# New issue-order tables for all five queues of a hybrid decoder step on one core

## The chip, the core and the metric

The kernel runs on one NeuronCore of one Trainium2 chip. The metric is device time in microseconds of one execution; a version is given by the median of its runs. Five engines with queues of their own work side by side: TensorE (PE in the profile), VectorE (DVE), ScalarE (ACT), GpSimd (POOL) and SyncE (SP), which here issues nearly all DMAs. Each works through its queue strictly in order: an instruction that waits for its input holds up everything behind it on that engine.

## The reference, cut to what matters

One layer of a decoder, in float32: 2048 prompt tokens and 8 single decode tokens, model width 1024.

```python
z = einsum(rmsnorm(x, norm1_g), w_in)            # 1024 -> 1792
xr, gr, q, k, v = split(z)
xc = causal_conv(xr)                             # width 4
hs = rglru(xc)                                   # gated linear recurrence, a scan over tokens
rec = hs * gelu(gr)
att = sliding_window_attention(q, k, v, sinks)   # window 128, 8 heads, 2 KV heads
mix = concat(rmsnorm(rec, rec_norm_g), rmsnorm(att, attn_norm_g))
h = x + einsum(mix, w_out)
hn = rmsnorm(h, norm2_g)
y = h + einsum(silu(einsum(hn, w_gate)) * einsum(hn, w_up), w_down)   # 1024 -> 2816 -> 1024
out = rmsnorm(y, final_norm_g)
```

Outputs are the normalized tokens, the last keys and values, and the states of convolution and recurrence.

## The kernel before

**Numbers.** Every product is made three times at TensorE's reduced-precision float32: high part by high part, high by low and low by high. So each operand exists as hi and lo: ACT casts the high part (for weights L1044, L1904, L1973), and POOL or DVE subtracts it from the original to get the low part (L1045, L1905, L1974). Activations get theirs the same way.

**Stage 1** (to about 650 us) takes the prompt in four sub-blocks of 520 and three times 512 tokens. For each: the norm (`xn`, L1106 and L1107), the input projection in 14 units of 128 columns (`ip`), the convolution (L1458), the recurrence with tanh gates (`g` on PE, `ra` and `ia` L1479 on ACT, then L1489 to L1501), the gelu gate (`gt`, L1518 to L1521), and attention: scores `s`, softmax (L1640 to L1651), transpositions of the probabilities `pt`, their hi and lo parts `pth` (ACT L1661) and `ptl` (DVE L1662), and the product `o`. The two group norms spread their factors over the partitions with small matmuls `bc_at` and `bc_rc`, whose result ACT copies out (`rb_at`, L1141); such a matmul needs the one PSUM bank for small things. The output projection `op` and the sums into the residual (`xres`, L1763) follow. ACT's square root and its exponential family live in different function tables, so a `ACT_TABLE_LOAD` stands between them.

**Stage 2** (from about 650 us) is the feed-forward part in three groups of tokens (2 × 344, 2 × 342, 2 × 342), each in 11 steps over slices of the hidden width. A step multiplies 2 × 2 blocks with seven products in place of eight, gate (`ps_g`), up (`ps_u`) and down (`pw`). Several products share a PSUM bank: before the next product may add to it, ACT (copies `c_u`, L2111, L2116, L2118) or DVE (`c_u`, L2090) must have read what is there. The sums into y are DVE's L2176. At a group's end comes the final norm: the row of factors is transposed on PE (`tr_f`), copied by ACT (L1150), written to HBM (`rows_f`, L1151) and read back spread over all partitions (`rb_f`, L1157); DVE multiplies y by it (L2196, 16 steps for a group), SP writes the result (`out_yT`, L2197), and the next group's y is loaded into the space that comes free (L1900). All of this runs while the next group's first products are on PE.

**The order.** The program is written as chains of steps, and each instruction is recorded under a key (the engine and the chain for DVE, ACT, POOL and SP, the PSUM tile for PE). A table of strings, `ORDER`, one string for each engine, then lists these keys in the order in which the engine shall issue them: `u2_1_5:12` is the next twelve matmuls of product 5 of the up part, group 2, step 1, and `pu1.1+1` is the second one still left of its chain. `order_engines()` reads the tables and ties each instruction to the one ahead of it, with no semaphore: only the order in the queue is bound.

```python
def order(runs, todo):
    last = None
    for run in runs.split():
        key, _, at = run.partition("+")
        key, _, n = key.partition(":")
        for _ in range(int(n or 1)):
            r = todo[key].pop(int(at or 0))
            if last is not None:
                tc.add_manual_dep(r, last.name, no_sync, reason="issue order")
            last = r
```

The data dependences, and the semaphores that come of them, are the same for every order. The tables also say how many warm-up matmuls stand in front (`w_st_x0:17`).

## Time and profile before

| | us |
|---|---|
| three runs | 2012.89, 2016.06, 2016.81 (median 2016.06) |
| the profiled execution | 2014.07 |
| its span, first to last instruction | 2012.3 |
| TensorE busy in it | 1981.0 (98%) |
| VectorE / ScalarE / GpSimd busy | 1562.8 / 979.2 / 960.3 |
| mean granted TensorE clock | 0.992 |

The profiled execution is one more than the three runs; it lies 1.99 us below their median. The page gives busy times, and names for each idle stretch of an engine what ended it ("<-DVE y L2176": a sum of VectorE at line 2176). Names there are those of the program without buffer numbers. The granted clock is that of TensorE; 1.00 is full speed. "PEld" is TensorE's loading of weights, which overlaps its products.

### The profile page before, as it was taken

What the parts mean: (1) busy time and instruction counts of PE and PEld (TensorE: products, weight loads), DVE (VectorE), ACT (ScalarE), POOL (GpSimd) and SP (SyncE); (2) the same over time, 40 slices, a digit from 0 to 9 for tenths busy, and PEclk for the clock granted to TensorE, in tenths of its full rate; (3) what the DMA queues carried; (4) which work ended last, traced back from release to release, by engine and by line L of the source; (5) the groups of instructions that cost most, each with busy time, mean ns of one, the idle gap of its engine ahead of it and who ended that gap; (6) DMA issues with size and microseconds to landing.
All of it is one profiled execution on the core that took longest, in us unless ns stands there. A gap on an engine that the chain in (4) does not pass through costs nothing.

```text
span 2012.3 us, 34843 instructions
## 1 busy us (share of the span) xinstructions
PE 1981.0 (98%) x12106; PEld 1882.1 (94%) x12106; DVE 1562.8 (78%) x2894; ACT 979.2 (49%) x2029; POOL 960.3 (48%) x822
## 2 busy tenths in 40 slices
PE   9999999999999999999999999999999999999997
PEld 9988888888877999999999999999999999999997
DVE  7877986777896889889888786886568586766775
ACT  6775674564663544444446433433345333433433
POOL 5512452130232886788889754544456423322323
PEclk9999999999999999999999999999999999999998
DMA  9864675586688978566668786776557775565552
GB/s 319 301 231 132 208 273 197 173 265 209 214 293 276 334 254 272 210 217 223 237 234 285 252 295 226 242 235 205 191 191 268 225 254 199 178 212 192 184 182 93
DMA packets 218471, 461.93 MB, mean 230 GB/s; under 512 B 26231, under 2 KB 90407, under 8 KB 218279
## 3 DMA queue, kind: packets, MB, share of 16 engines
q1 hardware_dynamic: 214662, 456.69, 67.8%
q10 hardware_dynamic: 3632, 3.02, 0.5%
q8 instruction: 95, 1.56, 0.3%
q14 instruction: 82, 0.66, 0.1%
HBM read 345.51 MB, written 115.17 MB: 229 GB/s over the span
## 4 chain that ended last, share of the span: by engine, by line
PE 91%; DVE 5%; DMA 2%; ACT 1%; issue 1%; POOL 0%; SPq 0%; DVEq 0%; ACTq 0%; POOLq 0%
PE ps_u L1071 21%; PE ps_g L1071 21%; PE pw L1071 18%; PE ip L1071 13%; PE op L1071 8%; PE pd L1071 4%; PE o L1071 1%; PE s L1071 1%; PE pt L1076 1%; PE g L1071 1%; DMA rb_f<-rows_f 0%; DVE y L2196 0%; DMA rb_x<-rows_x 0%; DVE xn L1107 0%; DVE y L2245 0%
## 5 line engine op out<-in xcount | busy, mean ns | idle before, releaser
L1071 PE MATMUL ps_g<-hn,w_g 128*128 128x342 f32 (+1 forms) x2772 | 570.2, 320 | 0.2 <-DVE c_u L2090 0.2
L1071 PE MATMUL ps_u<-hn,w_u 128*128 128x342 f32 (+1 forms) x2772 | 563.1, 321 | 3.3 <-ACT c_u L2111 3.2
L1071 PEld LDWEIGHTS ps_u<-hn,w_u 128*128 128x128 f32 x2772 | 462.6, 190 | 4.4 <-ACT c_u L2111 3.5
L1071 PEld LDWEIGHTS ps_g<-hn,w_g 128*128 128x128 f32 x2772 | 461.2, 188 | 1.6 <-issue 0.4
L2176 DVE TENSOR_TENSOR y<-y,pw 128x342 f32<-128x342 f32 (+1 forms) x756 | 358.5, 505 | 115.4 <-PE pw L1071 109.3
L1071 PE MATMUL ip<-xn,w_in 128*128 128x512 f32 (+1 forms) x1680 | 366.0, 358 | 2.5 <-ACT xn L1106 1.4
L1071 PEld LDWEIGHTS ip<-xn,w_in 128*128 128x128 f32 x1680 | 271.0, 190 | 43.3 <-ACT xn L1106 1.6
L1071 PE MATMUL pw<-fh,wd 128*128 128x342 f32 (+1 forms) x864 | 253.9, 320 | 0.1
L1071 PE MATMUL pw<-t,wd 128*128 128x342 f32 (+1 forms) x972 | 243.3, 320 | 4.6 <-DVE y L2176 3.9
L1071 PE MATMUL op<-mix,w_out 128*128 128x512 f32 (+1 forms) x960 | 208.4, 358 | 0.0
L1071 PEld LDWEIGHTS op<-mix,w_out 128*128 128x128 f32 x960 | 159.5, 191 | 24.7
L1071 PEld LDWEIGHTS pw<-t,wd 128*128 128x128 f32 x972 | 169.8, 188 | 6.1 <-DVE y L2176 5.1
L1974 POOL TENSOR_TENSOR wd<-rd,wd 128x512 fp32r<-128x512 f32 x85 | 121.0, 1423 | 101.9 <-ACT wd L1973 100.8
L1071 PEld LDWEIGHTS pw<-fh,wd 128*128 128x128 f32 x864 | 158.8, 189 | 0.9 <-DVE y L2176 0.3
L1973 ACT CAST wd<-rd 128x512 fp32r<-128x512 f32 x159 | 98.4, 620 | 120.4 <-PE ps_u L1071 44.2
L1905 POOL TENSOR_TENSOR w_u<-ru,w_u 128x512 fp32r<-128x512 f32 x44 | 60.5, 1375 | 172.1 <-ACT w_u L1904 156.9
L1071 PE MATMUL pw<-fl,wd 128*128 128x342 f32 (+1 forms) x432 | 132.7, 320 | 0.0
L2072 POOL TENSOR_TENSOR c_u<-c_u,c_g 128x342 f32<-128x342 f32 (+1 forms) x60 | 65.2, 1088 | 133.1 <-DVE c_u L2090 120.4
L2090 DVE TENSOR_TENSOR c_u<-c_u,ps_u 128x342 f32<-128x342 f32 (+1 forms) x99 | 50.3, 508 | 98.0 <-PE ps_u L1071 97.5
L2061 DVE TENSOR_TENSOR fl<-c_u,fh 128x342 fp32r<-128x342 f32 (+1 forms) x132 | 102.5, 781 | 17.4 <-ACT fh L2060 16.7
L2060 ACT CAST fh<-c_u 128x342 fp32r<-128x342 f32 (+1 forms) x132 | 63.1, 480 | 107.5 <-POOL c_u L2072 43.3
L1904 ACT CAST w_g<-rg 128x512 fp32r<-128x512 f32 x99 | 60.9, 621 | 70.9 <-issue 26.0
(319 smaller groups left out, 3528.2 us busy)
## 6 DMA issues: line engine op xcount, KB each, us to landing
w_g<-split_g SPq DMA_DIRECT2D x88, 512.0 KB, 4.3
w_u<-split_u SPq DMA_DIRECT2D x88, 512.0 KB, 4.6
w_in<-split_w SPq DMA_DIRECT2D x84, 512.0 KB, 3.7
rg<-in_wgate SPq DMA_DIRECT2D x110, 256.0 KB, 3.0
ru<-in_wup SPq DMA_DIRECT2D x110, 256.0 KB, 3.1
w_out<-split_w SPq DMA_DIRECT2D x48, 512.0 KB, 4.4
split_g<-w_g SPq DMA_DIRECT2D x44, 512.0 KB, 3.5
split_u<-w_u SPq DMA_DIRECT2D x44, 512.0 KB, 3.3
```

The source lines that it names most:

```text
L1071: r = nc.tensor.matmul(*args, **kw)
L1076: r = nc.tensor.transpose(*args)
L1904: nc.scalar.copy(w[:, 0, :], src)
L1905: lo_eng.tensor_tensor(w[:, 1, :], src, w[:, 0, :].bitcast(F32), op=ALU.subtract)
L1973: nc.scalar.copy(w[:, :, 0], v)
L1974: eng((E_DLO0, E_DLO1, E_DLO2)[gi][j]).tensor_tensor(w[:, :, 1], v, w[:, :, 0].bitcast(F32), op=ALU.subtract)
L2060: nc.scalar.copy(hi, v)
L2061: nc.vector.tensor_tensor(lo, v, hi.bitcast(F32), ALU.subtract)
L2072: (nc.vector if p == NPAIR - 1 or src is not v else eng(E_MUL[2 * h + n])).tensor_tensor(v, src, g, op=ALU.mult)
L2090: nc.vector.tensor_tensor(o, a, b, op)
L2176: nc.vector.tensor_tensor(v, v, ps, ALU.add)
```

## The change

Only the strings of `ORDER` are replaced, all five of them. The words that come with the change say that they were made with lengths out of four traces, with the table loads of ScalarE and the landings of factor rows (`rb_f` and the like) taken into account. Every instruction of before is there again; the new file is three lines shorter, so its line numbers are lower by three (L2108 is L2111 of before). Long stretches are in the same order as before, among them 150 to 200, 1000 to 1050 and 1200 to 1550 us on PE, and nearly all of the end. What moves lies in 0 to 100, 200 to 260, 550 to 700, 800 to 1000, 1090 to 1170 and about 1600 us.

Two lines of PE's string at about 1600 us, out of 166,000 characters of difference:

```diff
-g2_1_4:9 u2_1_2:11 tr_f1_0 u2_1_2 u2_1_6:12 w2_0_2_0:3 u2_1_7:11 u2_1_5:12 u2_1_7 w2_0_6_0:3 u2_1_4:12 u2_1_3:12
...
+g2_1_4:3 u2_1_1:11 g2_1_4:9 u2_1_2:11 tr_f1_0 u2_1_2 u2_1_6:12 w2_0_2_0:3 u2_1_7:11 u2_1_5:12 u2_1_7 u2_1_3:12
+u2_1_4:7 g2_2_1 u2_1_4 g2_2_1 u2_1_4:4 w2_0_6_1:3 w2_0_6_0:3 g2_2_1:7 w2_0_1_3:2 g2_2_2 w2_0_1_3 g2_2_1:2 g2_2_2
```

The strings themselves tell little; the rows below tell what stands in the queues.

**The border of the first and second group, about 1150 us.** ScalarE before; c_g and c_u are blocks of the gate and up part, ps_u1_1_1 is the bank that the up part's first product fills, wd and w_u are high parts of weights, t1 is a high part for the down product:

```order
L2069 ACTIVATE c_g1_1_10_7476<-ps_g1_1_1_13521 128x342
L2060 CAST t1_0_7472<-c_u1_0_11_7471 128x342
L2060 CAST t1_1_7473<-c_u1_0_10_7470 128x342
L1973 CAST wd1_0_4_13813<-sd0_4_13793 128x2x256
L1973 CAST wd1_0_3_13766<-rd1_0_3_13727 128x2x256
L2111 COPY c_u1_1_10_7488<-ps_u1_1_1_13752 128x342
L1973 CAST wd1_0_6_13902<-rd1_0_6_13772 128x2x256
L2116 COPY c_u1_1_01_7487<-ps_u1_1_1_13752 128x342
```

And after:

```order
L2066 ACTIVATE c_g1_1_10_7476<-ps_g1_1_1_13521 128x342
L2108 COPY c_u1_1_10_7488<-ps_u1_1_1_13752 128x342
L1970 CAST wd1_0_4_13813<-sd0_4_13793 128x2x256
L1970 CAST wd1_0_3_13766<-rd1_0_3_13727 128x2x256
L2057 CAST t1_1_7473<-c_u1_0_10_7470 128x342
L1970 CAST wd1_0_6_13902<-rd1_0_6_13772 128x2x256
L2113 COPY c_u1_1_01_7487<-ps_u1_1_1_13752 128x342
```

The copy of the first up product (c_u1_1_10, L2111, now L2108) moved from behind the casts of wd1_0_4 and wd1_0_3 to ahead of them, right behind the step that reads the gate's bank; the cast of t1_1 moved behind them.

VectorE at the same border before; y0_4 and so on are the first group's results, rb_f0_1 the row of factors of its second half:

```order
L2090 TENSOR_TENSOR c_g1_1_11_7477<-c_g1_1_11_7477,ps_g1_1_1_13521 128x342
L2196 SCALAR_TENSOR_TENSOR y0_4_8343<-y0_4_8343,vec_102,rb_f0_1_13615 128x344
L2196 SCALAR_TENSOR_TENSOR y0_1_8276<-y0_1_8276,vec_102,rb_f0_1_13615 128x344
L2196 SCALAR_TENSOR_TENSOR y0_3_8312<-y0_3_8312,vec_102,rb_f0_1_13615 128x344
L2196 SCALAR_TENSOR_TENSOR y0_5_8360<-y0_5_8360,vec_102,rb_f0_1_13615 128x344
L2196 SCALAR_TENSOR_TENSOR y0_1_8276<-y0_1_8276,vec_102,rb_f0_1_13615 128x344
L2196 SCALAR_TENSOR_TENSOR y0_1_8276<-y0_1_8276,vec_102,rb_f0_0_13645 128x344
L2090 TENSOR_TENSOR c_g1_1_01_7475<-c_g1_1_01_7475,ps_g1_1_5_13593 128x342
L2196 SCALAR_TENSOR_TENSOR y0_3_8312<-y0_3_8312,vec_102,rb_f0_0_13645 128x344
L2196 SCALAR_TENSOR_TENSOR y0_4_8343<-y0_4_8343,vec_102,rb_f0_0_13645 128x344 x2
L2196 SCALAR_TENSOR_TENSOR y0_3_8312<-y0_3_8312,vec_102,rb_f0_1_13615 128x344
```

And after:

```order
L2087 TENSOR_TENSOR c_g1_1_11_7477<-c_g1_1_11_7477,ps_g1_1_1_13521 128x342
L2058 TENSOR_TENSOR t1_0_7472<-c_u1_0_11_7471,t1_0_7472 128x342
L2058 TENSOR_TENSOR t1_1_7473<-c_u1_0_01_7469,t1_0_7472 128x342
L1902 TENSOR_TENSOR w_u1_1_2_13684<-ru1_1_01_13588,w_u1_1_2_13684 128x512
L2193 SCALAR_TENSOR_TENSOR y0_5_8360<-y0_5_8360,vec_102,rb_f0_1_13615 128x344
L2193 SCALAR_TENSOR_TENSOR y0_3_8312<-y0_3_8312,vec_102,rb_f0_1_13615 128x344
L2193 SCALAR_TENSOR_TENSOR y0_4_8343<-y0_4_8343,vec_102,rb_f0_1_13615 128x344
L2193 SCALAR_TENSOR_TENSOR y0_1_8276<-y0_1_8276,vec_102,rb_f0_1_13615 128x344
L2193 SCALAR_TENSOR_TENSOR y0_3_8312<-y0_3_8312,vec_102,rb_f0_1_13615 128x344
L2087 TENSOR_TENSOR c_g1_1_01_7475<-c_g1_1_01_7475,ps_g1_1_5_13593 128x342
L2193 SCALAR_TENSOR_TENSOR y0_1_8276<-y0_1_8276,vec_102,rb_f0_1_13615 128x344
L2193 SCALAR_TENSOR_TENSOR y0_1_8276<-y0_1_8276,vec_102,rb_f0_0_13645 128x344
```

Three steps (the low parts t1_0, t1_1 and w_u1_1_2) now stand ahead of the first multiplication by rb_f0_1; before, they stood behind 11 (t1_1), 12 (w_u1_1_2) and 14 (t1_0) of these multiplications, below the piece shown. The sum c_g1_1_01 comes after five of the multiplications instead of six.

**The recurrence of the second sub-block, about 250 us.** ScalarE before; the two table loads are those for the square root (L1496) and back to tanh and exponentials (L1479), ra1_2 is the tanh gate that frees the bank of g1_2:

```order
L1470 CAST xch1_2_3046<-xc1_2_2940 128x512
L1044 CAST w_out0_4_1_3372<-raw_out0_4_1_3370 128x512
L1117 ACTIVATE sq_h0_2_3431<-xres0_2_3234 128x520
L1044 CAST w_out0_5_0_3436<-raw_out0_5_0_3434 128x512
L1673 COPY ratt_150<-o5_0_2964 64x4x128
L1661 CAST pth5_1_0_2500<-pt5_1_0_2495 128x512
L1044 CAST w_out0_5_1_3442<-raw_out0_5_1_3440 128x512
L1620 CAST qst7_1_2607<-qraw_148 64x512
L1479 ACT_TABLE_LOAD
L1479 ACTIVATE ra1_2_3044<-g1_2_0_0_3050,hab_154 128x512
```

And after:

```order
L1467 CAST xch1_2_3046<-xc1_2_2940 128x512
L1670 COPY ratt_150<-o5_0_2964 64x4x128
L1658 CAST pth5_1_0_2500<-pt5_1_0_2495 128x512
L1103 ACTIVATE xn2_5_3680<-xs2_5_3678,vec_102 128x512
L1114 ACTIVATE sq_h0_2_3431<-xres0_2_3234 128x520
L1041 CAST w_out0_5_0_3436<-raw_out0_5_0_3434 128x512
L1476 ACT_TABLE_LOAD
L1476 ACTIVATE ra1_2_3044<-g1_2_0_0_3050,hab_154 128x512
L1103 ACTIVATE xn2_6_3685<-xs2_6_3683,vec_102 128x512
L1041 CAST w_out0_5_1_3442<-raw_out0_5_1_3440 128x512
L1617 CAST qst7_1_2607<-qraw_148 64x512
```

The casts of w_out0_5_1 and qst7_1 moved from ahead of the second table load to behind the tanh; the square sq_h0_2 and the cast of w_out0_5_0 moved behind the copies of the attention unit (L1673 and L1661, now L1670 and L1658).

**The border of the second and third group, about 1605 us.** TensorE before; pw2_0_1_0 is a bank of the down product, w_u2_1_3 and w_u2_1_4 are weights of the third and fourth product of the up part:

```order
L1071 MATMUL ps_u2_1_5_18816<-hn2_1_2_17945,w_u2_1_5_18714 128x342 x3
L1071 MATMUL ps_u2_1_1_18695<-hn2_1_4_17961,w_u2_1_7_18754 128x342
L1071 MATMUL pw2_0_1_0_18675<-t2_0_7652,wd2_0_1_18624 128x342 x3
L1071 MATMUL ps_u2_1_1_18695<-hn2_1_8_18012,w_u2_1_4_18833 128x342 x4
L1071 MATMUL ps_u2_1_1_18695<-hn2_1_9_18021,w_u2_1_4_18833 128x342
L1071 MATMUL ps_u2_1_1_18695<-hn2_1_8_18012,w_u2_1_4_18833 128x342
L1071 MATMUL ps_u2_1_1_18695<-hn2_1_9_18021,w_u2_1_4_18833 128x342 x3
L1071 MATMUL ps_u2_1_1_18695<-hn2_1_10_18043,w_u2_1_4_18833 128x342 x3
L1071 MATMUL ps_u2_1_5_18816<-hn2_1_5_17980,w_u2_1_3_18794 128x342 x3
```

And after:

```order
L1068 MATMUL ps_u2_1_5_18816<-hn2_1_2_17945,w_u2_1_5_18714 128x342 x3
L1068 MATMUL ps_u2_1_1_18695<-hn2_1_4_17961,w_u2_1_7_18754 128x342
L1068 MATMUL ps_u2_1_5_18816<-hn2_1_5_17980,w_u2_1_3_18794 128x342 x3
L1068 MATMUL ps_u2_1_5_18816<-hn2_1_6_17987,w_u2_1_3_18794 128x342 x4
L1068 MATMUL ps_u2_1_5_18816<-hn2_1_7_17991,w_u2_1_3_18794 128x342
L1068 MATMUL ps_u2_1_5_18816<-hn2_1_6_17987,w_u2_1_3_18794 128x342
L1068 MATMUL ps_u2_1_5_18816<-hn2_1_7_17991,w_u2_1_3_18794 128x342 x3
L1068 MATMUL ps_u2_1_1_18695<-hn2_1_8_18012,w_u2_1_4_18833 128x342 x4
L1068 MATMUL ps_u2_1_1_18695<-hn2_1_9_18021,w_u2_1_4_18833 128x342
L1068 MATMUL ps_u2_1_1_18695<-hn2_1_8_18012,w_u2_1_4_18833 128x342
L1068 MATMUL ps_u2_1_1_18695<-hn2_1_9_18021,w_u2_1_4_18833 128x342
```

The twelve matmuls with w_u2_1_3 and the twelve with w_u2_1_4 now stand ahead of the three of pw2_0_1_0, which follow seven rows below the piece shown.

## The prediction

> **What bounds the kernel now.** I read the page's head first, then what TensorE (PE) waited for, then fifty-microsecond windows, and last the timeline around each wait.

> ```profile
> span 2012.3 us, 34843 instructions
> PE 1981.0 (98%) x12106; PEld 1882.1 (94%) x12106; DVE 1562.8 (78%) x2894; ACT 979.2 (49%) x2029; POOL 960.3 (48%) x822
> ```

> TensorE is busy for 1981.0 of 2012.3 us. The change keeps all instructions, so it can only win from the 31.3 us in which PE has nothing to do, and from time at a lowered clock. PE's waits, with total, number and longest:

> ```profile
> PE pw L1071 <- DVE y L2176: 3.9, 2, 3.2
> PE ps_u L1071 <- ACT c_u L2111: 3.2, 1, 3.2
> PE g L1071 <- ACT ra L1479: 2.7, 1, 2.7
> ...
> PE pt L1076 <- DVE ptl L1662: 1.8, 2, 1.6
> PE bc_at L1071 <- ACT rb_at L1141: 1.8, 1, 1.8
> PE ip L1071 <- ACT xn L1106: 1.4, 1, 1.4
> ```

> Five of these lie in the middle of the run, each at one place with at most a small second one; the last is the start. The windows show the place and the clock (columns: window, length, busy time of PE, PEld, DVE, ACT, POOL with counts, granted PE clock, DMA share, GB/s):

> ```profile
> 200.00:250.00 50.00, 48.25 (x313) 43.56 (x311) 46.45 (x73) 35.88 (x68) 20.14 (x18) 0.97 0.61 206
> 250.00:300.00 50.00, 47.06 (x320) 43.16 (x319) 41.80 (x81) 37.42 (x76) 25.40 (x25) 0.97 0.79 271
> 600.00:650.00 50.00, 47.70 (x219) 38.14 (x218) 31.54 (x54) 20.48 (x42) 10.57 (x8) 0.97 0.83 269
> 1150.00:1200.00 50.00, 45.95 (x277) 44.53 (x276) 43.47 (x85) 17.02 (x35) 29.32 (x28) 0.97 0.90 297
> 1600.00:1650.00 50.00, 46.70 (x287) 46.09 (x286) 39.41 (x80) 16.36 (x33) 12.53 (x12) 0.97 0.84 275
> 1154.70:1158.10 3.40, 3.40 (x14) 3.40 (x13) 3.40 (x6) 0.29 (x1) 1.28 (x1) 0.50 0.98 357
> 1158.20:1161.60 3.40, 3.40 (x24) 3.40 (x23) 3.40 (x9) 1.76 (x5) 0.00 (x0) 1.00 0.92 237
> ```

> The last two rows give a second price. Behind the wait at 1153.8 PE ran 14 matmuls in 3.40 us at clock 0.50, and 24 in the next 3.40 us at 1.00. Ten matmuls fewer, at 0.14 us each, are 1.4; half of 3.4 is 1.7; I take **1.6 us for each slow stretch**. Each of the five windows at 0.97 holds one, since 3% of 50 us is 1.5; in the first of them the only wait of size is the 1.8 us of bc_at. So a stall at one of these places costs its wait plus 1.6. [...] The last microseconds I take as unchanged: the order there is the same but for a few rows.

> **Part by part.** First the group boundary at 1150, place D. DVE, ACT, PE and SyncE's queue there:

> ```profile
> 1148.69 2.99 DVE L2196 SCALAR_TENSOR_TENSOR y<-y,vec,rb_f 128x344 f32<-128x344 f32 x5 [5.11 <-DMA rb_f<-rows_f]
> 1157.74 0.50 DVE L2061 TENSOR_TENSOR t<-c_u,t 128x342 fp32r<-128x342 f32 x1
> 1152.30 0.62 ACT L1973 CAST wd<-sd 128x512 fp32r<-128x512 f32 x1 [2.55 <-POOL sd L2006]
> ...
> 1153.34 0.44 ACT L2111 COPY c_u<-ps_u 128x342 f32<-128x342 f32 x1
> 1153.83 1.09 PE L1071 MATMUL ps_u<-hn,w_u 128*128 128x342 f32 x5 [3.19 <-ACT c_u L2111]
> 1163.90 0.58 PE L1071 MATMUL pw<-t,wd 128*128 128x342 f32 x2 [0.76 <-DVE y L2176]
> 1158.73 2.27 SPq L1900 DMA_DIRECT2D y<-hs  x4
> ```

> PE waited 3.19 us for a copy of 0.44 us that stood on ACT behind two casts, the first of which waited 2.55 us for POOL. In the new order the copy stands ahead of both. Its input, the first u product, had been issued by then, as PE stood idle behind it, so the copy is done about when PE asks for it at 1150.64 (1153.83 − 3.19): the wait and its slow stretch go, 3.19 + 1.6 = 4.8. What is late next: DVE's rank of L2196 steps, 16 of about 0.6 us (2.99 for five), begins only when rb_f lands, and y of the next group can only be loaded when they have left. The three small DVE steps that are now put ahead of them fill the 5.11 us of idle and cost nothing; uncovered, they would cost about 0.5 each (the L2061 row). But the landing itself does not move: 4.3 us from issue, in all four cases.

> ```profile
> DMA to landing us min/median/max: 4.3/4.3/4.3
> ```

> PE reaches the product that waited at 1163.90 about 4.8 us earlier, at 1158.4 (1163.90 − 0.76 − 4.8); the loads of y started at 1158.73 and can move up by perhaps 3 us, because DVE does its L2196 steps in one run. I expect a wait there of 2.0 instead of 0.76. D: 4.8 − 1.2 = **3.6** (0 if that wait grows to 4 us with a slow stretch; 5.5 if it vanishes).

> Place B, at 257, is ACT again:

> ```profile
> 251.35 0.64 ACT L1117 ACTIVATE sq_h<-xres 128x520 f32<-128x520 f32 x1 [3.46 <-DVE xres L1763]
> 253.62 0.62 ACT L1044 CAST w_out<-raw_out 128x512 fp32r<-128x512 f32 x1
> 254.90 1.28 ACT L1479 ACT_TABLE_LOAD   x1
> 256.19 0.69 ACT L1479 ACTIVATE ra<-g,hab 128x512 f32<-128x512 f32 x1
> ```

> Two casts (from 253.62 to 254.90, 1.28 us) move behind the table load and the tanh; that alone brings the tanh to 254.9. The 3.46 us of idle ahead of them were a wait for a residual sum of DVE, which the new order does before two other DVE steps. Together PE, which waited 2.7, has perhaps 0.3 left: 2.4 + 1.6 = **4.0** (1.3 with the casts alone and the slow stretch kept; 4.3 at most). The cost is that the second half of a w_out weight is ready about 2 us later on POOL; PE reads it units later.

> Place A, at 218, is less than it looks:

> ```profile
> 212.37 3.54 DVE L1521 SCALAR_TENSOR_TENSOR rrec<-gt,rrec 128x512 f32<-128x512 f32 x1
> 215.94 0.63 ACT L1518 ACTIVATE gt<-rrec 128x512 f32<-128x512 f32 x1 [3.75 <-DVE rrec L1521]
> 212.85 2.51 POOL L1045 TENSOR_TENSOR w_out<-raw_out,w_out 128x512 fp32r<-128x512 f32 x2
> L1521 DVE SCALAR_TENSOR_TENSOR rrec<-gt,rrec x16: 676/686/3536, 98.4 to 572.2; 128x512 f32<-128x512 f32 x12, 128x520 f32<-128x520 f32 x4
> ```

> The factor copy (rb_at) now goes ahead of two ACT steps of 0.6, but it still stands behind L1518, whose wait came from a DVE step that ran 3.54 instead of 0.69 us while POOL worked on two weights. POOL's order there is unchanged. One more DVE step even stands between. A: **0.3** (−1 to 1.8 + 1.6 = 3.4). [...]

> Place E, at 1608:

> ```profile
> 1600.49 0.63 SPq L1157 DMA_DIRECT2D rb_f<-rows_f  x1
> 1605.40 1.92 DVE L2196 SCALAR_TENSOR_TENSOR y<-y,vec,rb_f 128x342 f32<-128x342 f32 x2 [6.38 <-DMA rb_f<-rows_f]
> 1607.80 0.74 PE L1071 MATMUL pw<-t,wd 128*128 128x342 f32 x3 [3.17 <-DVE y L2176]
> w_u<-split_u SPq DMA_DIRECT2D x88, 512.0 KB, 4.6
> ```

> PE stood for 3.17 us, from 1604.6 to 1607.8, for a y sum queued behind rb_f. The new order gives PE 26 other matmuls first: 12 of product 3, then 12 of product 4 and 2 of the next pair. Product 3 needs its weight, which is now issued right behind rb_f, at about 1601.2, and flies for 4.6 us: 1605.8, a wait of 1.2. Product 4 accumulates in a bank that DVE must read first (L2090), now behind four L2196 steps: 1605.40 + 1.92 for two + 2 × 0.6 + 0.5 = 1609.0, while PE gets there at 1605.8 + 12 × 0.157 = 1607.7 (estimated above the 3.4 / 24 = 0.142 of the window quoted, which 0.142 would make 1607.5): another 1.3. So about 2.5 of 3.2 stays as two shorter waits; with some chance that no slow stretch follows them I take **0.8** (0 to 4.8).

> The attention passes at 606 (waits of 1.6 and 0.2 for ptl, one slow stretch) are reordered on PE, DVE and ACT: a transposition goes ahead of an o product and eight output products go into the gap, but an ACT copy (mix L1545) now stands ahead of a cast that PE waits for. **0.5** (−1.5 to 3.4). The start: ACT's first cast and first xn no longer stand behind a small step that waited for the vectors, so I let the wait of 1.4 shrink by 0.6: **0.6** (0 to 2).

> Against this stand the many small reorderings of the first 650 us, on a DVE that is nearly full where they lie:

> ```profile
> 540.00:600.00 60.00, 59.46 (x292) 48.47 (x291) 54.20 (x116) 39.99 (x80) 19.66 (x19) 1.00 0.85 274
> ```

> PE lost only 0.5 us in these 60, because DVE, 54.20 busy, was just in time. There a new order can hardly win and can lose. I set **−1.8** for it: one new wait of about 0.2 with its slow stretch, or two of 0.9 without (0 to −12.8, below). Sum: 3.6 + 4.0 + 0.3 + 0.8 + 0.5 + 0.6 − 1.8 = **8.0 us**. The profiled run took 2014.07 (its span 2012.3 and 1.8 outside), so its like would take 2006.1. The median of the three runs, 2016.06, lies 2.0 above it; the forecast for the median is 2016.06 − 8.0 = 2008.1, rounded to **2008**.

> **The rivals.** *First: the waits only move (no change).* At D and E the L2196 steps and the loads of y behind them stay where the landing of rb_f puts them; PE comes 4.8 us sooner and waits as much longer at the product of 1163.90, at clock 0.50 again. For it: 4.3 us of flight in all four cases and DVE's 43.47 of 50 in that window. Against it: DVE's idle of 5.11 us now takes work out of that rank. Then D and E give 0, and 4.0 + 0.3 + 0.5 + 0.6 − 1.8 = 3.6 is left: 2016.06 − 3.6 = 2012.5, within 0.2% (4 us, about what a measurement of this kernel can tell from no change).

> *Second: slower, through DVE's queue in the attention of the last sub-block.* The step and its reader on PE before:

> ```profile
> 549.13 0.69 DVE L1662 TENSOR_TENSOR ptl<-pt,pth 128x512 fp32r<-128x512 f32 x1
> 559.57 0.48 PE L1071 MATMUL o<-ptl,vt 128*128 128x512 f32 x1
> ```

> The ptl step (L1662) of this half unit ran ten microseconds before PE needed it. In the new order it stands some 18 DVE steps later, behind a scan (L1501), a product (L1509) and the four L1651 of the next unit; at 54.20 / 116 = 0.47 us each that is 8.5 us, so it ends at about 558.3, close to where PE wants it. All later halves go through the same single score and output banks. From the point where it comes 1.6 us late (as the ptl wait at 606 did), each of the six halves of units 13 to 15 waits that long: 9.6, with two slow stretches 3.2, together 12.8 in place of the 1.8 set above. If the gain of B is lost as well, because the residual sum is late again, the balance is 3.6 + 0.3 + 0.8 + 0.5 + 0.6 − 12.8 = −7.0: 2023. With B kept it is −3.0: 2019. Against it: in the whole run PE waited 1.8 us for ptl steps, in two places, though every unit goes through the same kind of pass.

> *Third: nothing happens,* because the tables bind only the issue order and PE's work is the same to the instruction. The five waits are plainly queue waits, so this would need all of them to be landings: 2016.

> **How the numbers follow.** Forecast 0.60 (faster by over 0.2%); first rival 0.25 and third 0.03 (within); second 0.12 (slower). Hence 0.60, 0.28, 0.12. The range for 8 in 10: below, D, B and E at their best ends add 1.9 + 0.3 + 4.0, and the attention passes another 2.9: 9.1 less, 1999. Above, it takes in the first rival's 2012.5 and the milder form of the second, to 2018.5. The forecast's own range is 2000 to 2012.

> **What would show it.** Right: no wait ps_u <- c_u L2111 in the list of waits, and no row of clock 0.97 at 1150; g <- ra L1479 below 0.5; pw <- y L2176 still there, at 1150 to 1165 and in parts at 1605 to 1610; bc_at <- rb_at still over 1. The windows at 540 to 600 lose no more than 2 us of PE. Wrong: a new row of o or pt <- ptl with more than 3 us in all; or pw <- y above 6 us, the first rival; or all waits gone and DVE idle, then my landings were too late and the time is near 1999.

## The result, and the profile after

| | runs | median, us | ratio to before, 95% interval |
|---|---|---|---|
| before | 2012.89 to 2016.81 (4) | 2015.59 | |
| new tables | 2004.64, 1999.68, 1998.70, 2000.69 | 2000.18 | 0.9929 (0.9910 to 0.9948) |

Faster by 0.71%, between 0.52 and 0.90 (before has the three runs of the prediction and one more). The forecast was 2008, its range 1999 to 2018.5: the sign held, the time lies near the low end, and the gain, some 14 us by the ratio, is nearly twice the 8.0 that was forecast. The profiled execution of the new kernel is the longest of its four, 2004.64, so from profile to profile 9.4 us are won (2014.07 − 2004.64), and 15.4 between the medians. Both differences have to be explained. The page's head and TensorE's waits after (total, times, longest):

```profile
span 2002.6 us, 34828 instructions
PE 1975.7 (99%) x12106; PEld 1879.2 (94%) x12106; DVE 1561.5 (78%) x2894; ACT 977.8 (49%) x2029; POOL 961.7 (48%) x822
```

```profile
PE ps_u L1068 <- DMA w_u<-split_u: 4.2, 2, 3.8
...
PE pw L1068 <- DVE y L2173: 1.4, 3, 0.6
...
PE pw L1068 <- DVE wd L1971: 1.1, 1, 1.1
PE tr_f L1073 <- DVE cols_f L1123: 1.0, 1, 1.0
PE o L1068 <- DVE ptl L1659: 1.0, 1, 1.0
...
PE bc_at L1068 <- ACT rb_at L1138: 0.6, 1, 0.6
...
PE bc_f L1068 <- DVE cols_f L2226: 0.6, 1, 0.6
PE pt L1073 <- DVE ptl L1659: 0.5, 1, 0.5
```

The waits for c_u (D) and ra (B) are gone, bc_at (A) fell from 1.8 to 0.6, y from 3.9 to 1.4. In their place stand one for a weight (3.8, at E), and new ones for wd and cols_f. The windows of places A, B, the attention passes (two), D and E; E comes eight microseconds earlier now, so its window begins at 1590 in place of 1600:

```profile
200.00:250.00 50.00, 49.40 (x332) 44.99 (x332) 48.93 (x79) 38.33 (x70) 21.11 (x17) 1.00 0.61 217
250.00:300.00 50.00, 50.00 (x343) 45.42 (x342) 39.64 (x83) 37.46 (x81) 28.37 (x30) 1.00 0.87 297
540.00:600.00 60.00, 57.31 (x274) 45.77 (x273) 52.24 (x111) 38.08 (x78) 19.30 (x20) 0.97 0.82 266
600.00:650.00 50.00, 49.42 (x231) 40.27 (x230) 31.45 (x55) 19.73 (x40) 14.27 (x11) 1.00 0.88 296
1150.00:1200.00 50.00, 47.43 (x285) 45.82 (x284) 40.36 (x81) 14.65 (x30) 27.34 (x26) 0.97 0.87 282
1590.00:1640.00 50.00, 46.05 (x282) 45.42 (x281) 39.48 (x83) 15.74 (x32) 13.35 (x11) 0.97 0.80 266
```

Place E in the timeline, SyncE's issue of the weight behind rb_f and TensorE's wait for it:

```profile
1593.12 0.33 SPq L1154 DMA_DIRECT2D rb_f<-rows_f  x1
1593.54 0.38 SPq L1925 DMA_DIRECT2D w_u<-split_u  x1
1599.46 4.76 PE L1068 MATMUL ps_u<-hn,w_u 128*128 128x342 f32 x19 [3.83 <-DMA w_u<-split_u]
```

A and B lost their slow stretch (clock 1.00 instead of 0.97); D, E and the attention passes still have one, in the passes before 600 us now instead of behind it.

Where the time went is seen best by TensorE's own progress: both kernels run the same 12106 matmuls, so I took from the traces when the n-th one starts, and how much later or earlier that is than in the profiled execution of before, section by section (limits in times of before; minus is a gain; the last section runs to the end of the span):

| section | forecast | new kernel | its second profiled execution |
|---|---|---|---|
| 0 to 195, start | −0.6 | +0.3 | +0.4 |
| 195 to 235, A | −0.3 | −2.7 | −2.7 |
| 235 to 300, B | −4.0 | −4.8 | −4.8 |
| 300 to 620, attention and reorderings | +1.3 | 0.0 | +0.7 |
| 620 to 1100 | 0 | −2.3 | −2.7 |
| 1100 to 1200, D | −3.6 | +0.6 | +1.2 |
| 1200 to 1590 | 0 | 0.0 | +0.7 |
| 1590 to 1650, E | −0.8 | +0.7 | +0.4 |
| 1650 to the end | 0 | −1.5 | −1.5 |
| sum | −8.0 | −9.7 | −8.4 |

A and B give 7.5 of 9.7; both borders of the second stage, forecast at 4.4 together, give nothing.

### The profile page after: what moved, and what is told of

The parts are those of the page before. It is cut to its first block, busy times and chain, and to the rows that moved or that the text cites. A ratio compares the mean times of both kernels' runs of the same rounds, so it can differ in the third digit from the quotient of the medians.

```text
span 2002.6 us, 34828 instructions
## 1 busy us (share of the span) xinstructions
PE 1975.7 (99%) x12106; PEld 1879.2 (94%) x12106; DVE 1561.5 (78%) x2894; ACT 977.8 (49%) x2029; POOL 961.7 (48%) x822
## 4 chain that ended last, share of the span: by engine, by line
PE 88%; DMA 5%; DVE 3%; POOL 2%; ACT 1%; issue 1%; SPq 0%; ACTq 0%; DVEq 0%; POOLq 0%
PE ps_g L1068 20%; PE ps_u L1068 20%; PE pw L1068 18%; PE ip L1068 14%; PE op L1068 7%; PE pd L1068 3%; PE s L1068 1%; PE o L1068 1%; PE pt L1073 1%; PE g L1068 1%; DMA n<-hs 1%; POOL hn L1252 1%; DMA mixed<-n 0%; DMA ru<-in_wup 0%; DMA rows_f<-row_f 0%
## 5 line engine op out<-in xcount | busy, mean ns | idle before, releaser
L2173 DVE TENSOR_TENSOR y<-y,pw 128x342 f32<-128x342 f32 (+1 forms) x756 | 360.0, 506 | 117.2 <-PE pw L1068 110.4
L2058 DVE TENSOR_TENSOR fl<-c_u,fh 128x342 fp32r<-128x342 f32 (+1 forms) x132 | 106.3, 812 | 19.6 <-ACT fh L2057 19.0
## 6 DMA issues: line engine op xcount, KB each, us to landing
w_g<-split_g SPq DMA_DIRECT2D x88, 512.0 KB
w_u<-split_u SPq DMA_DIRECT2D x88, 512.0 KB
w_in<-split_w SPq DMA_DIRECT2D x84, 512.0 KB
w_out<-split_w SPq DMA_DIRECT2D x48, 512.0 KB
split_g<-w_g SPq DMA_DIRECT2D x44, 512.0 KB
split_u<-w_u SPq DMA_DIRECT2D x44, 512.0 KB
```

Of the source, the lines that this page charges most:

```text
L2058: nc.vector.tensor_tensor(lo, v, hi.bitcast(F32), ALU.subtract)
L2173: nc.vector.tensor_tensor(v, v, ps, ALU.add)
```

## The experiments

Theory: each place is an order in a queue; what a table frees there it keeps, and the sections add up. Rival: what is freed comes back as a wait for something that did not move (the landings of rb_f and of weights, y). Nine kernels test one place each and one tests A and B together; the new kernel was also run again, and the last kernel joins the moves.

**A and B alone** (the kernel before with the new order from 160 to 400 us only). The core of it on ScalarE:

```diff
-L1044 CAST w_out0_5_1_3442<-raw_out0_5_1_3440 128x512
-L1620 CAST qst7_1_2607<-qraw_148 64x512
 L1479 ACT_TABLE_LOAD
 L1479 ACTIVATE ra1_2_3044<-g1_2_0_0_3050,hab_154 128x512
+L1044 CAST w_out0_5_1_3442<-raw_out0_5_1_3440 128x512
+L1620 CAST qst7_1_2607<-qraw_148 64x512
```

> The kernel before, with the new order on all five queues only between about 160 and 400 us (places A and B). Theory 1 (each place gains what its own queues free, and keeps it): in the trace of the new kernel TensorE is 2.6 us ahead of the old one more behind A than ahead of it, 4.3 more behind B and 0.5 more up to 300, so about 7.4 less here, 0.37%; g <- ra is gone, bc_at <- rb_at is about 0.6, and no slow stretch stands between 200 and 300. The terms of the prediction (A 0.3, B 4.0): 4.3 less, with bc_at <- rb_at above 1 and its slow stretch still there. Rival (a gain made ahead of the busy VectorE at 540 to 600 is given back there): TensorE is 7 us ahead at 300, and no more than 3 at 620.

2007.19 (2005.76 to 2009.61), ratio 0.9956 (0.9941 to 0.9971): 8.9 us less, 6 to 12. TensorE's waits have no row for ra any more, and this for A:

```profile
PE bc_at L1072 <- ACT rb_at L1142: 0.6, 1, 0.6
```

By progress A gives 2.8 and B 4.6. Between 540 and 620 this execution falls back by 3.0, but so do E alone and the end alone, by 2.8 and 3.0, which have the old order up to there: that is not the gain given back (below, at 590). Most of the change is A and B: 7.3 of 9.7 us by progress, 8.9 of some 14 by the times.

**D alone** (new order from 1060 to 1400 only; the rows are those of the section on the change).

```diff
+L2111 COPY c_u1_1_10_7488<-ps_u1_1_1_13752 128x342
 L1973 CAST wd1_0_4_13813<-sd0_4_13793 128x2x256
 L1973 CAST wd1_0_3_13766<-rd1_0_3_13727 128x2x256
-L2111 COPY c_u1_1_10_7488<-ps_u1_1_1_13752 128x342
```

> The kernel before, with the new order only between about 1060 and 1400 us (place D, the border of the first and second group). Theory 1 (the wait for c_u, 3.2 with its slow stretch, is traded for a wait of tr_f for cols_f of 1.2 and for four short waits for wd, y and w_u behind it, 3.7 in all with a slow stretch of their own): within 1 us of before at 1200, so no difference that shows. The prediction's term: 3.6 less, 0.18%, with one wait of 2.0 for y. Rival (the short waits of the new kernel's trace come from places ahead of this one, by which TensorE arrives 8 us early for loads that do not move): then this kernel has none of them and is 4 us or more faster.

2018.04 (10 runs), ratio 1.0001 (0.9991 to 1.0011): nothing. The wait for c_u is gone, and these have come:

```profile
PE pw L1071 <- DVE y L2176: 4.5, 4, 3.3
...
PE pw L1071 <- DVE wd L1974: 1.1, 1, 1.1
...
PE tr_f L1076 <- DVE cols_f L1126: 1.0, 1, 1.0
```

(The 3.3 is E's.) The short waits come with D's own order, not from an early TensorE. By progress TensorE first loses 1.05, at tr_f, then gains 4.9 up to 1158 us, and by 1170 it has given back 4.1.

**E alone** (new order from 1400 to 1700 only). SyncE's part of it:

```diff
+L1157 DMA rb_f_0_18589<-rows_f_0_18583 128x342
+L1928 DMA w_u_1_3_18794<-split_u 128x1024
...
-L1157 DMA rb_f_0_18589<-rows_f_0_18583 128x342
...
-L1928 DMA w_u_1_3_18794<-split_u 128x1024
```

> The kernel before, with the new order only between about 1400 and 1700 us (place E, the border of the second and third group). Theory 1 (product 3 of the up part is ahead of its weight, whose load is queued behind that of rb_f): a wait of 3 to 4 us for w_u with a slow stretch, no wait for y, and a time 0 to 1 us above before's. The prediction's term: 0.8 less, with two waits of 1.2 and 1.3. Rival (the wait of 4.0 in the trace of the new kernel belonged to that execution alone, in which the load took 5.9 instead of 4.6 us): a wait of about 1.2 for w_u without a slow stretch, and 3 us less than before.

2017.12 (10 runs), ratio 1.0001 (0.9991 to 1.0011), and by progress +0.4 at E. The wait for y is replaced by one for the weight:

```profile
PE ps_u L1071 <- DMA w_u<-split_u: 3.5, 1, 3.5
```

It is no accident of one execution: every table with this order shows 3.2 to 4.0 there.

**The end alone** (new order behind 1700 us).

```diff
+L2229 RECIPROCAL cols_f_0_22909<-cols_f_0_22909 114x3
 L2245 SCALAR_TENSOR_TENSOR y_3_18622<-y_3_18622,vec,bc_f_1_22836 128x342 x2
 L2245 SCALAR_TENSOR_TENSOR y_4_18648<-y_4_18648,vec,bc_f_1_22836 128x342
 L2245 SCALAR_TENSOR_TENSOR y_5_18665<-y_5_18665,vec,bc_f_1_22836 128x342
-L2229 RECIPROCAL cols_f_0_22909<-cols_f_0_22909 114x3
```

> The kernel before, with the new order only behind about 1700 us (15 places in the queues of VectorE, ScalarE and SyncE). Theory 1 (the reciprocals of the last column factors stand ahead of four instead of behind eight multiplications on VectorE): bc_f <- cols_f falls from 2.3 to 0.6, 1.4 to 1.8 us less at the end, which is below what the times can tell and has to be seen in the profile. The prediction's term for the end: 0. Rival: the end is set by the last result's transfer, and TensorE's earlier bc_f changes the span by less than 0.5.

2015.77 (10 runs), ratio 0.9993 (0.9984 to 1.0003). The times cannot tell it, the profile can: 1.5 less behind 1650 by progress, with the second of these rows in place of the first:

```profile
PE bc_f L1071 <- DVE cols_f L2229: 2.3, 1, 2.3
PE bc_f L1071 <- DVE cols_f L2229: 0.6, 1, 0.6
```

**The new kernel again**, unchanged.

> The new kernel once more, unchanged, for a second profiled execution. Its first profiled execution took 2004.64, its three other runs 1998.7 to 2000.7. Theory 1 (the wait of 4.0 us for w_u at 1595 with the slow stretch behind it, 5.6 together, differs between executions, because the load had taken 5.9 us there instead of 4.6): an execution of about 2000 shows that wait at 1.5 to 2.5 us and no slow stretch at 1600. Theory 2 (the difference lies elsewhere, or in all places a little): the wait is 4 again in an execution of 2000.

Runs 2005.68, 2006.26, 2003.82, 1999.25 (ratio 0.9933, 0.9916 to 0.9949). The profiled one, 2005.68, has E's wait at 3.5 and the same stretch behind it. As it is a long execution again, this run does not tell the theories apart; the other profiles do: variants with E untouched and short executions (2000.11 below) have that wait too. So theory 1 fell. The eight runs lie in two groups, 1998.7 to 2000.7 and 2003.8 to 2006.3; the median of all is 2002.3.

A part of what differs between executions is seen at 590. VectorE and GpSimd in the first profiled execution of the new kernel:

```profile
577.00 0.58 DVE L1195 SCALAR_TENSOR_TENSOR n<-n,vec,hb 128x344 f32<-128x344 f32 x1 [2.00 <-DMA n<-hs]
586.61 1.64 DVE L1203 TENSOR_TENSOR n<-n,n 128x344 f32<-128x344 f32 x1
588.18 1.37 DVE L1648 TENSOR_SCALAR sc<-sc,mx 128x256 f32<-128x256 f32 x1
586.59 1.29 POOL L1115 TENSOR_TENSOR rcacc<-rcacc,sq_rc 128x512 f32<-128x512 f32 x1
587.84 1.56 POOL L1115 TENSOR_TENSOR hacc<-hacc,sq_h 128x512 f32<-128x512 f32 x1
```

And in that of the variant at A (last but one below), whose queues at this place are the same:

```profile
574.95 0.57 DVE L1195 SCALAR_TENSOR_TENSOR n<-n,vec,hb 128x344 f32<-128x344 f32 x1 [0.92 <-DMA n<-hs]
584.55 0.52 DVE L1203 TENSOR_TENSOR n<-n,n 128x344 f32<-128x344 f32 x1
584.98 0.35 DVE L1648 TENSOR_SCALAR sc<-sc,mx 128x256 f32<-128x256 f32 x1
585.64 1.30 POOL L1115 TENSOR_TENSOR rcacc<-rcacc,sq_rc 128x512 f32<-128x512 f32 x1
```

In the new kernel L1203 started 0.02 us behind GpSimd's step and took three times as long; where it started 0.8 us or more ahead of that step it was not stretched (0.52 in the variant at A). Both profiled executions of the new kernel have this collision; its five variants below, other than the next, have not. It is VectorE that comes at another time: counted from the same matmul of TensorE at 580, GpSimd's step begins within 0.4 us in all of them, and L1203 1.1 to 2.1 us later in the two with the collision. A wait some ten microseconds earlier goes with it: VectorE stood 2.00 and 2.25 us for the load of n in these two, 0.35 to 1.26 in the five. Why that load lands later in some executions is open.

By progress the five without the collision are 3.0 to 3.6 further at 600. But a slow stretch follows in four of them, at 598 to 600 (the new kernel has its own, at 593 and 594), and by 620 only 1.5 to 1.9 of the lead are left; the fifth has no slow stretch there and keeps 3.5. Nor does every execution without it belong to the short group: two of the five took 2003.3 and 2003.6. So the collision is worth 1.5 to 3.5 us and is not shown to make the two groups. The start is another part: up to 195 us these executions lie up to 1.7 us apart. The profiled executions of the old order differ here too: those of A and B alone, E alone and the end alone lose 2.8 to 3.0 between 540 and 620 against that of before, though none of the three has a new order there.

**The collision avoided by order:** three VectorE steps moved.

```diff
-L1195 SCALAR_TENSOR_TENSOR n_3_1_5635<-n_3_1_5635,vec,hb_1_5493 128x344
-L1195 SCALAR_TENSOR_TENSOR n_3_0_5638<-n_3_0_5638,vec,hb_0_5491 128x344
-L1203 TENSOR_TENSOR n_3_1_5635<-n_3_1_5635,n_3_0_5638 128x344
...
 L1659 TENSOR_TENSOR ptl_1_1_6872<-pt_1_1_6866,pth_1_1_6871 128x512
 L1760 TENSOR_TENSOR xres_6_6330<-xres_6_6330,op_6_0_6460 128x512
+L1195 SCALAR_TENSOR_TENSOR n_3_1_5635<-n_3_1_5635,vec,hb_1_5493 128x344
+L1195 SCALAR_TENSOR_TENSOR n_3_0_5638<-n_3_0_5638,vec,hb_0_5491 128x344
+L1203 TENSOR_TENSOR n_3_1_5635<-n_3_1_5635,n_3_0_5638 128x344
```

> The new kernel with three steps moved on VectorE at about 586 us (two L1195 and the L1203, parts of the next stage's input): they stand behind the scores of the next half unit, its ptl and a residual sum instead of ahead of them. In the two executions of the new kernel that took 2004.6 and 2005.7 the step L1203 started 0.02 us after a step of GpSimd (L1115) and took 1.64 instead of 0.52, and the L1648 behind it 1.37 instead of 0.35; three executions of its variants had GpSimd a microsecond later, no stretch, and were 3.3 us further at 600. Theory 1 (that collision is what makes the new kernel's times lie between 1998.7 and 2006.3): the steps beside L1115 are now scores, which read PSUM and are not stretched; the waits at 592 to 594 go, in the profile and in nearly all times, which then lie at 1999 to 2002. Rival (it is late for another reason, the collision only goes along with it): the wait for ptl at 592 stays over 1 us in a part of the executions, and the times spread as before.

2008.32 (2006.50 to 2009.26), ratio 0.9949 (0.9931 to 0.9967): slower than the new kernel, by some 4 us going by the ratios and 6 by the medians. The collision is gone as theory 1 said (L1203 takes 0.52), and so is the wait for ptl at 592. But the edit had a cost that I had not counted:

```profile
590.45 0.52 DVE L1203 TENSOR_TENSOR n<-n,n 128x344 f32<-128x344 f32 x1
597.04 0.52 DVE L1252 TENSOR_TENSOR hn<-m,hn 128x344 fp32r<-128x344 f32 x1 [4.48 <-ACT hn L1251]
596.53 0.48 ACT L1251 CAST hn<-m 128x344 fp32r<-128x344 f32 x1 [6.37 <-DMA m<-mixed]
598.27 0.66 PE L1073 MATMUL pt<-cs,sc 128*128 128x128 f32 x4 [2.93 <-DVE ptl L1659]
```

The moved steps feed a store (mixed) and a load (m) whose cast stands on ScalarE ahead of the probabilities' copy: coming late, they stopped ScalarE for 6.37 us and TensorE for 2.93, and three slow slots follow, from 599 to 609. The spread (2.8) is smaller than the new kernel's 7.6, but with four runs that is no proof.

**ScalarE's part of B alone** (the diff of the first experiment, nothing else moved).

> The kernel before with one edit, on ScalarE at place B: the casts of w_out0_5_1 and qst7_1 stand behind the table load and the tanh ra1_2 instead of ahead of them. Theory 1 (the casts are 1.28 us of a wait of 2.9, the rest is the residual sum that VectorE makes late, as the prediction split it): a wait of about 1.6 for ra at 257; 1.3 us less, or 2.9 if a wait of that length has no slow stretch behind it (one of 1.2 had none in these runs, those of 1.8 and 1.9 had). Rival (ScalarE's own queue is all of it): the wait is below 0.5 and 4 us are won.

2015.36 (10 runs), ratio 0.9987 (0.9977 to 0.9997): 2.6 less, 0.6 to 4.6.

```profile
PE g L1071 <- ACT ra L1479: 1.5, 1, 1.5
```

2.7 became 1.5: the casts are 1.2 of it, as in the prediction's split, and no slow stretch follows. The rest of B the prediction laid to the residual sum; no run moves that alone. By progress this execution is 2.7 ahead at 262 us and 0.9 at 300.

**E, the weight earlier, then also the sum.** First SyncE's load alone, then with VectorE's step:

```diff
 L1925 DMA w_u_1_5_18714<-split_u 128x1024
+L1925 DMA w_u_1_3_18794<-split_u 128x1024
...
 L1154 DMA rb_f_0_18589<-rows_f_0_18583 128x342
-L1925 DMA w_u_1_3_18794<-split_u 128x1024
```

```diff
+L2087 TENSOR_TENSOR c_u_1_11_7669<-c_u_1_11_7669,ps_u_1_1_18695 128x342
 L2193 SCALAR_TENSOR_TENSOR y_1_13591<-y_1_13591,vec,rb_f_0_18589 128x342
 L2193 SCALAR_TENSOR_TENSOR y_3_13678<-y_3_13678,vec,rb_f_0_18589 128x342
 L2193 SCALAR_TENSOR_TENSOR y_4_13703<-y_4_13703,vec,rb_f_0_18589 128x342 x2
-L2087 TENSOR_TENSOR c_u_1_11_7669<-c_u_1_11_7669,ps_u_1_1_18695 128x342
```

> The new kernel with one load moved on SyncE: that of w_u2_1_3 (the weight of the up part's product 3 at place E) stands five rows earlier, right behind that of w_u2_1_5 and ahead of rows_f1_0 and rb_f1_0. Theory 1 (that load's place behind rb_f makes the wait at 1595): it is issued at about 1588 instead of 1593.5, lands before 1595.5, and the wait of 4.0 and its slow stretch go; 4 to 5.6 us less than the first profiled execution of the new kernel, and 0 to 5.6 less than its median. Rival (the bank that VectorE must read, the second of the two waits that the prediction put there, or y, then stops TensorE for as long): no change, with a new wait for c_u or y of 2 to 4 us at 1596 to 1600.

> The new kernel with the earlier load of w_u2_1_3 (as in the run before) and one step moved on VectorE: the sum c_u2_1_11, which reads the bank that product 4 of the up part needs, stands ahead of the first multiplication by rb_f1_0 instead of behind four of them. In the run with the load alone TensorE waited 1.2 for w_u and then 3.0 for that sum, while VectorE stood idle for 6.8 us in front of rb_f1_0. Theory 1 (place E is an order of queues on two engines, one behind the other): the second wait goes too, the slow stretch at 1600 with it; TensorE is 3 to 5 us further at 1606 than in the new kernel, 0.15 to 0.25% in the time. Rival (the first rival of the prediction: y of the next group, behind the multiplications, then stops TensorE): a wait for y of 2 to 4 us at 1600 to 1605, and no gain.

The load alone: 2004.15, ratio 0.9932 (0.9917 to 0.9947). Both: 2002.17, ratio 0.9921 (0.9898 to 0.9945). Neither is told apart from the new kernel by its times. TensorE in the first, then in the second:

```profile
1596.03 2.13 PE L1068 MATMUL ps_u<-hn,w_u 128*128 128x342 f32 x12 [1.06 <-DMA w_u<-split_u]
1601.04 1.35 PE L1068 MATMUL ps_u<-hn,w_u 128*128 128x342 f32 x7 [2.88 <-DVE c_u L2087]
```

```profile
1600.60 0.74 PE L1068 MATMUL pw<-t,wd 128*128 128x342 f32 x3 [2.05 <-DVE y L2173]
1601.99 0.74 PE L1068 MATMUL pw<-t,wd 128*128 128x342 f32 x3 [0.65 <-DVE y L2173]
```

The wait is handed on: weight, then sum, then y. Against the new kernel's profiled execution the first gains 3.8 us by progress up to 1602 and has lost them all by 1606; the second gains 4.9 up to 1604, of which 3.3 are back by 1606 and 0.45 is left at 1620. The rival holds in the main: behind rb_f stands a chain that no single move shortens. VectorE waits 6.76 for rb_f in the first and 2.91 in the second, then does the rank.

**D, the step of wd earlier**, ahead of the low part's four multiplications.

```diff
+L1971 TENSOR_TENSOR wd_0_3_13766<-rd_0_3_13727,wd_0_3_13766 128x2x256
 L2003 TENSOR_TENSOR sd_5_13837<-rd_0_3_13727,rd_0_8_13769 128x256
...
 L2193 SCALAR_TENSOR_TENSOR y_2_8294<-y_2_8294,vec,rb_f_0_13645 128x344
-L1971 TENSOR_TENSOR wd_0_3_13766<-rd_0_3_13727,wd_0_3_13766 128x2x256
```

> The new kernel with one step moved on VectorE: the low part of wd1_0_3 at place D stands nine rows earlier, ahead of the step of sd0_5, so no longer behind four multiplications by rb_f. Theory 1 (the short waits that took the place of c_u's are queue waits on VectorE and not landings): the wait of 1.2 at 1152 goes, the waits for y behind it stay near 0.75 each, and with less idle time the slow stretch at 1156 may go: 1.2 to 2.9 us less. Rival (the loads of y set this stretch, as the first rival of the prediction had it): the waits for y grow by what the wait for wd loses, no change.

2002.57 (2000.11 to 2006.23), ratio 0.9933 (0.9916 to 0.9949). The wait for wd went, those for y grew from 1.4 to 2.6: the rival. By progress 1.6 us are gained here, 1.2 of them by the slow stretch, which went.

```profile
PE pw L1068 <- DVE y L2173: 2.6, 3, 1.2
```

**A, GpSimd's two steps later.**

```diff
+L1442 COPY xr_3_2875<-hist 128x3
+L1468 TENSOR_TENSOR xcl_1_2895<-xc_1_2802,xch_1_2894 128x512
 L1042 TENSOR_TENSOR w_out_0_0_3110<-raw_out_0_0_3108,w_out_0_0_3110 128x512
 L1042 TENSOR_TENSOR w_out_0_1_3116<-raw_out_0_1_3114,w_out_0_1_3116 128x512
-L1442 COPY xr_3_2875<-hist 128x3
-L1468 TENSOR_TENSOR xcl_1_2895<-xc_1_2802,xch_1_2894 128x512
```

> The new kernel with two steps moved on GpSimd at place A: the low parts of w_out0_0 and w_out0_1 stand behind the copy of xr and the step of xcl instead of ahead of them. Theory 1 (VectorE's step L1518, 0.69 us elsewhere and 3.96 here, is held by the two steps of GpSimd that run beside it): it takes about 0.7 at 211.4, the chain behind it comes 3 us sooner, and the wait of 0.6 of bc_at for rb_at goes; 0.6 us or nothing less in the time. Rival (it is long for another reason, a wait or the small atcols step of GpSimd right ahead): it takes over 2 us again. Against both: TensorE may wait for the low parts of w_out, which come 3 us later, at 222.

2003.20 (2001.18 to 2003.58), ratio 0.9928 (0.9913 to 0.9943). VectorE's step and GpSimd's in the new kernel, then the step in this one:

```profile
211.39 3.96 DVE L1518 SCALAR_TENSOR_TENSOR rrec<-gt,rrec 128x512 f32<-128x512 f32 x1
212.27 2.53 POOL L1042 TENSOR_TENSOR w_out<-raw_out,w_out 128x512 fp32r<-128x512 f32 x2
```

```profile
211.48 0.69 DVE L1518 SCALAR_TENSOR_TENSOR rrec<-gt,rrec 128x512 f32<-128x512 f32 x1
```

3.96 became 0.69, the wait of bc_at is gone, and TensorE gains 0.85: theory 1. The small atcols step of GpSimd still ran beside it and did no harm. (In the records the two steps begin 0.9 behind L1518, so behind its usual 0.69; how they come to stretch it is not shown.)

**Together:** these moves, the column factors at 1131 one step earlier, and sums into y ahead of one multiplication at D and of three at E.

> The new kernel with the edits that took a wait away, together: GpSimd's two steps at A, the step of wd1_0_3 and two sums into y ahead of one multiplication by rb_f0 at D, the column factors cols_f0_0 ahead of a sum at 1131, the load of w_u2_1_3 and the sum c_u2_1_11 at E, and there also the first sum into y2_0 two multiplications earlier than in the run with these two (three earlier than in the new kernel). Theory 1 (each wait is an order in a queue and what replaces it is smaller): A 0.9, the wait at 1131 1.2, D 1.2 to 2, E 1 to 3 with no slow stretch at 1156 and 1600; together 4 to 7 us below the new kernel's execution of the same kind, so a median of 1995 to 1999. Rival (the first rival of the prediction holds at both borders: multiplications and y only take over what is removed): A and 1131 alone, 2 us, 2000 to 2002. Nothing here touches the collision at 586 that makes some executions 3.3 us longer.

1999.64 (1998.24 to 2002.36, 5 runs), ratio 0.9916 (0.9902 to 0.9929): 2.6 below the median of the new kernel's eight runs, intervals overlapping, so not shown to be faster. Against the variant at D (an execution of the same kind) only 0.9 is won: the 1.0 won at 1131 came back at once as a longer wait for a weight, and E's wait stands at y.

```profile
1146.14 1.66 PE L1068 MATMUL ps_u<-hn,w_u 128*128 128x342 f32 x9 [1.58 <-DMA w_u<-split_u]
1599.54 0.74 PE L1068 MATMUL pw<-t,wd 128*128 128x342 f32 x3 [2.11 <-DVE y L2173]
```

## Why the prediction was right, and which terms were not

The sign was right because the waits at A and B were what the prediction took them for, orders in queues, and behind them no other late thing stopped TensorE for long. That the sum came out near is partly luck: D and E, forecast at 4.4, gave nothing, and A, the end and the stretch from 620 to 1100, forecast at 0.3 together, gave 6.5. Of the signs that it named, the waits for c_u and ra went and short ones for y stayed at D, as said; but E had no wait for y left, the window of clock 0.97 at 1150 stayed, bc_at fell below 1, and TensorE lost 2.7 us in the window from 540 to 600, not at most 2.

**B, 4.0: right.** 4.8 measured. The tanh at 256.19 now runs at 251.01, and TensorE does not wait:

```profile
251.01 0.69 ACT L1476 ACTIVATE ra<-g,hab 128x512 f32<-128x512 f32 x1
```

Of these five microseconds some 2.5 had been gained ahead of B and 2.7 are the wait; the casts gave 1.2 of it, as split.

**A, 0.3: mis-sized.** The reason given held: VectorE's step (L1521 before, L1518 now) was stretched again, to 3.96, and the wait did not vanish. But the prediction had named two ScalarE steps of 0.6 that rb_at passes and hardly counted them. Before, rb_at started 2.1 us behind ScalarE's gt, now 0.5 behind it:

```profile
218.03 0.48 ACT L1141 COPY rb_at<-bc_at 128x416 f32<-128x416 f32 x1
```

```profile
216.71 0.63 ACT L1515 ACTIVATE gt<-rrec 128x512 f32<-128x512 f32 x1
217.24 0.49 ACT L1138 COPY rb_at<-bc_at 128x416 f32<-128x416 f32 x1
```

(The gt of before is the row at 215.94 in the prediction.) TensorE also got a transposition ahead of the second bc_at. So 1.8 became 0.6, and the slow stretch went with it: 2.7 in all; the upper end was 3.4. That GpSimd's two steps stretch L1518, the run at A shows: 3.96 with them beside it, 0.69 without.

**D, 3.6: failed**, and the first rival was right in its outcome, nothing gained, though not in the one long wait that it named. The step that failed is "a wait there of 2.0 instead of 0.76". The wait for c_u went as said. But the low part of wd1_0_3 stands behind four multiplications of the rank; tr_f lost 1.0 to cols_f, which the prediction left out; and instead of one wait of 2.0 there are five short ones with a slow stretch of their own: 4.9 gained, 4.1 and 1.0 lost in D alone.

**E, 0.8: failed in size.** Both waits that I named are there, one behind the other. For the weight I took 4.6 of flight from an issue at 1601.2 and got 1.2. The load is issued only 2.1 before TensorE stops (1599.46 − 3.83 − 1593.54) and not 3.4, as rb_f in front of it did not come earlier by as much as TensorE did, and it takes 5.9: hence 3.8. The second, 1.3 in the forecast, is hidden behind the first and shows as 2.9 when that goes.

**The start, 0.6: not there.** The wait for ACT's xn fell from 1.4 to 0.7, but TensorE then waited 1.6 for VectorE's half of xn (0.4 before) and 0.8 for w_in (0.3 before): 0.3 lost.

**The reorderings, −1.8: wrong sign.** Nothing was lost between 300 and 620 (0.0, and 1.6 to 3.5 won in the five variants without the collision), and 2.3 won between 620 and 1100, 1.4 of it from 800 to 850, where a wait for t (L2061 of before, 0.5) is gone; I had no term there, and can place no more of it. The second rival (ptl late six times) did not occur; ptl waits are 1.5 in all.

**The end, 0: wrong.** I took it as unchanged "but for a few rows"; one of these rows is the reciprocal in front of bc_f, 1.5 us.

**The profile and the median.** I added 2.0 to go from the profiled execution to the median. The new kernel's profiled execution lies 2.4 above the median of its eight runs: before's was one without the loss at 540 to 620, the new one's a long one. Of the 13 to 15 us between the medians, 9.4 are in the two profiles. The collision is some 1.5 to 3.5 of the rest, if the short runs of the new kernel are without it, which was not profiled; the remainder is open.

## What to carry to other kernels

A wait removed from TensorE is worth its length only up to the next thing that did not move: before counting it, look up what TensorE asks for next and when that lands (here y behind rb_f, twice). Count every step that comes out from between a cause and its waiter, not only the step at the head of the chain, and read the last microseconds of the order as closely as the middle. A moved step has readers far away: follow it through its store and load.

## What the runs showed of the hardware that was not expected

```profile
216.03:219.44 3.41, 1.66 (x9) 1.09 (x8) 2.71 (x5) 2.85 (x7) 1.76 (x2) 1.00 0.96 355
219.44:222.85 3.41, 3.41 (x11) 2.74 (x10) 2.72 (x4) 1.54 (x3) 2.19 (x3) 0.50 0.46 133
```

```profile
217.70:221.11 3.41, 1.87 (x9) 1.60 (x10) 2.81 (x4) 2.25 (x6) 2.76 (x2) 1.00 0.82 287
221.11:224.52 3.41, 3.41 (x24) 3.06 (x23) 2.71 (x3) 1.84 (x3) 2.09 (x3) 1.00 0.61 196
```

1.75 idle in the slot: clock 0.50 in the next. 1.54, as a part fell into the slot ahead: 1.00, and by progress 1.0 us saved with the same code. Over the 14 profiles, between 200 and 300 and from 1100 to 1980 us, all 20 slots with 1.87 us of idle or more were followed by a slow one, of the 19 from 1.30 to 1.85 eight were, below 1.30 one, and that was slow itself. Elsewhere less was enough: at 595, in the attention passes, four profiles have a slow slot behind one with 0.99 to 1.26 us of idle. So idle time by the records is not all that counts. The prediction's fixed 1.6 for each stretch was thus a matter of phase; in D alone A and B lost theirs with no edit there, 2.2 us.

**Which steps collide.** Counted in the new kernel's trace: of the 88 steps fl L2058 that are 342 wide (both inputs in SBUF) 29 took over 0.25 us more than their median of 0.51, each with GpSimd at work beside it, while another 23 had it beside them for over half of their time and were not stretched; of the 756 sums y L2173, which read PSUM, 378 had GpSimd beside them for over half of their time and none was stretched. So where a step of VectorE has to stand next to GpSimd's work, a sum that reads PSUM is the one that lost nothing by it in this trace.
